# A decoder trunk's expert layer: 256 instead of 128 tokens gather their experts' rows, and wq, u and v are multiplied as plain float32

## The chip, the cores and the metric

One core of one Trainium2 chip runs the whole program. The metric is the device time of one execution in microseconds. The core has TensorE (PE, with its weight loads shown apart as PEld), VectorE (DVE), ScalarE (ACT), GpSimd (POOL), SyncE (SP) and 16 DMA engines that serve the queues of SP, ACT and POOL.

## The reference, cut to what matters

512 tokens of width 1024 go through two mixers (a gated recurrence and a sparse attention), then through the expert layer below, with an RMSNorm at the end. Each token picks, in each of 8 heads, 16 of 16384 experts; an expert is one row of u and one row of v.

```python
def block(xb):                                   # 128 tokens
    q = (xb @ w_q).reshape(TB, H, 2, PEER_HALF)  # 1024 -> 8 x 2 x 128
    s = jnp.einsum('thpc,phnc->thpn', q, sub_keys)
    s1, i1 = lax.top_k(s[:, :, 0], K)            # K = 16 of 128
    s2, i2 = lax.top_k(s[:, :, 1], K)
    cand = (s1[..., :, None] + s2[..., None, :]).reshape(TB, H, K * K)
    ...
    top_s, pos = lax.top_k(cand, K)
    eidx = ...                                   # i1 * 128 + i2 at pos: 128 experts a token
    g = jax.nn.softmax(top_s, axis=-1).reshape(TB, H * K)
    h = jnp.einsum('tkd,td->tk', u[eidx], xb)
    a = jax.nn.gelu(h, approximate=False) * g
    return jnp.einsum('tk,tkd->td', a, v[eidx])
```

## The kernel before

The mixers and the output projection take the first 465 us; they are the same in both kernels but for the last copies of the normalized activations. The expert layer follows, in two ways at once.

**Dense, for three blocks of 128 tokens (384 tokens).** Chunk j holds the 128 experts i * 128 + j. `u_chunk` loads the chunk of u (128 x 1024 float32, on SP's queue), multiplies it with the activations of all 384 tokens into one PSUM tile, and a Gelu writes h. `g_block` and `g_group` build the weight of every expert for every token from one-hot matrices (`oz`, `ow`), 8 tokens a group; each 32 tokens are written to HBM (`g_d`, on SP's queue). `v_parts` loads the chunk of v (ACT's queue) and the g of the chunk (one read serves QJ chunks), multiplies g and h to `aj`, and `v_product` adds aj times v into six PSUM accumulators (3 blocks x 2 halves of the width) that stay open to the end.

**Gathered, for block 0 (128 tokens).** `row` has POOL issue an indirect DMA, which fetches one row of 1024 float32 for each of 128 tokens. `u_row` multiplies it with the token and sums on DVE, `v_row` adds the weighted row of v to `acc` on DVE. 128 rows of u come before 128 rows of v. The row buffers (`gp`, 4 of them) let POOL run ahead of DVE by as many rows.

**Split products.** Most matmuls before are float32r products of two parts: `weight` loads a float32 tile, ACT casts a high part, DVE subtracts it for a low part, and `mm3` issues three matmuls (high x high, high x low, low x high). Products of plain float32 tiles, such as the scores of `scores`, are one call.

**Order.** The instructions of each engine stay in the order of the program. For each head: two `query` calls, UH[h] u chunks, the scores, then `picks` (top 16 on DVE). Next, u chunks up to LEAD with the groups of g between them. Then an iteration for each remaining chunk: u of chunk q + AHEAD, v of chunk q; after these, iterations with v alone for the first LEAD chunks, whose h was kept in HBM (`h_d`) till then. `some_rows` spreads the row operations: R0 for each u chunk in the heads, R1 while g is built, R2 in an iteration with u and v, R3 in one with v alone. It places them on DVE behind the instruction that `pace[0]` names; POOL takes them in the same order. `some_rows` takes rows of u only for heads that have picked. The last two chunks (`lasts`) come after all rows; `total` and `finish` add the residual, normalize and write.

Of the kernel before, what the change touches and what calls it, by code (L numbers as in the profile page):

```python
# [40 lines left out]
def trunk(ctx, tc, A, out, dbg=None):  # L41
# [41 lines left out]
    wst = ctx.enter_context(tc.tile_pool(name="wst", reuse_waits="tile", bufs=2))  # L83
# [504 lines left out]
    def norm_ffn(b):
        xf = xf0 if b == 0 else nf.tile([P, D], F32, name="xf")
# [41 lines left out]
    dve.tensor_copy(io16k, iota[:, :, None].to_broadcast([P, 16, 16]))  # L631

    def query(m, w=S):

        hi, lo = cut(weight(A["peer_wq"][m]), 8)
# [34 lines left out]
    def picks(h, sc2):  # L670
# [38 lines left out]
        dve.scalar_tensor_tensor(eidx[:, hs], e12[:, 0, 0], 128.0, e12[:, 1, 0], op0=OP.mult, op1=OP.add)  # L709
        for z in range(2):  # L710
            act.copy(iw12[:, :, z, hs], e12[:, z, 1:, :])

    def weigh():
# [7 lines left out]
        for b in range(NB):  # L721
            o = gw0 if b == 0 else iw12[:, b - 1, 2, :]
# [7 lines left out]

    LEAD, UH, AHEAD = 76, [3] * 7 + [7], 2
    UPRE = sum(UH)
    R0, R1, R2, R3, NOROW = 0, 1, 2.9, 0.95, 8
    TG, QJ = 32, 4
    NG = NT // TG
    g_d = dram.tile([NG, P, P, TG], F32, name="g_d")
# [12 lines left out]
    gp = ctx.enter_context(tc.tile_pool(name="gp", reuse_waits="tile", bufs=4))  # L749
    wk = ctx.enter_context(tc.tile_pool(name="wk4", reuse_waits="tile", bufs=2))  # L750
    hh = wk.tile([P, P], F32, name="hh", bufs=1)
    ah = wk.tile([P, P], F32, name="ah", bufs=1)
    scr = wk.tile([P, D], F32, name="scr", bufs=1)

    def row(tab, k):
        g = gp.tile([P, D], F32, name="row")
        pool.indirect_dma_start(out=g, out_offset=None, in_=A[tab],  # L757
                                in_offset=bass.IndirectOffsetOnAxis(ap=eidx[:, k:k + 1], axis=0))
        return g

# [12 lines left out]

    rows = list(range(P))
# [12 lines left out]

    vrows = []
    for h in range(8):
# [3 lines left out]
        for i, j in enumerate(range(sum(UH[:h]), sum(UH[:h + 1]))):  # L793
# [3 lines left out]
            some_rows(R0, h * 16)  # L797
# [7 lines left out]
    vt = ctx.enter_context(tc.tile_pool(name="vt", reuse_waits="tile", bufs=2))  # L805
    with ExitStack() as st:
# [8 lines left out]
        TB = 8  # L815
# [241 lines left out]
```

## Time and profile before

| | |
|---|---|
| time, median of 3 runs | 1710.43 us (1709.58 to 1716.81) |
| the profiled execution | 1711.65 us, of which the span of the profile is 1709.9 us |
| TensorE busy | 1675.5 us |
| DVE busy | 1340.8 us |
| ACT, POOL busy | 729.3 us, 377.0 us |
| moved by DMA | 414.9 MB |
| mean granted TensorE clock | 0.996 |

Busy times of TensorE come from modelled ends of pipelined matmuls: neighbours overlap, so what one costs in a row of many is the distance between two starts, not its length. The DMA share is the mean busy share of the 16 engines; GB/s is what they moved in the stretch.

### The profile page before, as it was taken

What the parts mean: (1) busy time and instruction counts of PE and PEld (TensorE: products, weight loads), DVE (VectorE), ACT (ScalarE), POOL (GpSimd) and SP (SyncE); (2) the same over time, 40 slices, a digit from 0 to 9 for tenths busy, and PEclk for the clock granted to TensorE, in tenths of its full rate; (3) what the DMA queues carried; (4) which work ended last, traced back from release to release, by engine and by line L of the source; (5) the groups of instructions that cost most, each with busy time, mean ns of one, the idle gap of its engine ahead of it and who ended that gap; (6) DMA issues with size and microseconds to landing.
All of it is one profiled execution on the core that took longest, in us unless ns stands there. A gap on an engine that the chain in (4) does not pass through costs nothing.

```text
span 1709.9 us, 24687 instructions
## 1 busy us (share of the span) xinstructions
PE 1675.5 (98%) x9095; PEld 1465.9 (86%) x9097; DVE 1340.8 (78%) x2573; ACT 729.3 (43%) x1052; POOL 377.0 (22%) x284
## 2 busy tenths in 40 slices
PE   8999999999999999999999999999999999999997
PEld 6988887777798888999999999999999978888886
DVE  4776887547699999998988588878887888877785
ACT  4322226734443434566666433333333333333333
POOL 2000000000010000232322144444444442333320
PEclk9999999999999999999999999999999999999999
DMA  7321233127454334798988899999999999999983
GB/s 234 131 81 50 75 125 116 56 94 241 163 177 128 126 123 131 248 359 316 359 316 336 278 338 335 337 331 319 322 317 344 324 336 353 357 333 346 321 299 131
DMA packets 172472, 414.90 MB, mean 243 GB/s; under 512 B 14744, under 2 KB 85784, under 8 KB 170688
## 3 DMA queue, kind: packets, MB, share of 16 engines
q10 hardware_dynamic: 101072, 141.70, 24.4%
q1 hardware_dynamic: 34416, 137.40, 22.6%
q0 software_dynamic: 36864, 134.23, 22.4%
q8 instruction: 71, 1.16, 0.3%
q14 instruction: 49, 0.40, 0.1%
HBM read 366.86 MB, written 49.04 MB: 243 GB/s over the span
## 4 chain that ended last, share of the span: by engine, by line
PE 41%; issue 33%; DMA 11%; POOL 9%; DVE 5%; ACT 1%; POOLq 0%; SPq 0%; ACTq 0%; DVEq 0%
POOL row L757 8%; PE acc L79 6%; PE acc L77 6%; PE acc L78 6%; DMA row<-in_peer_u,eidx 5%; PE ps_mm L77 5%; PE ps_mm L79 5%; PE ps_mm L78 5%; DMA row<-in_peer_v,eidx 4%; PE ps_hg L379 2%; PE ps_hg L77 1%; PE ps_yb L460 1%; PE ps_hg L78 1%; PE ps_hg L79 1%; DMA v_raw<-in_peer_v 1%
## 5 line engine op out<-in xcount | busy, mean ns | idle before, releaser
L108 ACT CAST w_hi<-w_raw 128x1024 fp32r<-128x1024 f32 (+2 forms) x215 | 219.2, 1020 | 401.0 <-PE ps_u L78 125.4
L110 DVE TENSOR_TENSOR w_lo<-w_raw,w_hi 128x1024 fp32r<-128x1024 f32 (+2 forms) x215 | 254.9, 1185 | 84.4 <-ACT w_hi L108 72.1
L757 POOL DMA_INDIRECT row<-in_peer_u,eidx x128 | 178.5, 1394 | 553.6 <-DVE hh L762 503.6
L77 PE MATMUL ps_u<-xfH,w_hi 128*128 128x384 f32 x800 | 274.0, 343 | 1.4 <-ACT hg L744 1.4
L78 PE MATMUL ps_u<-xfL,w_hi 128*128 128x384 f32 x800 | 270.6, 338 | 0.0
L79 PE MATMUL ps_u<-xfH,w_lo 128*128 128x384 f32 x800 | 269.9, 337 | 0.0
L757 POOL DMA_INDIRECT row<-in_peer_v,eidx x128 | 178.6, 1395 | 275.5 <-DVE acc L772 253.3
L78 PE MATMUL acc<-v_lo,aH 128*128 128x512 f32 x540 | 211.2, 391 | 3.3 <-DVE v_lo L895 3.3
L77 PE MATMUL acc<-v_hi,aH 128*128 128x512 f32 x540 | 212.1, 393 | 1.4 <-ACT aH L906 1.1
L79 PE MATMUL acc<-v_hi,aL 128*128 128x512 f32 x540 | 212.1, 393 | 0.1
L906 ACT CAST aH<-aj 128x384 fp32r<-128x384 f32 x128 | 65.6, 513 | 308.7 <-DVE aj L903 138.1
L772 DVE SCALAR_TENSOR_TENSOR acc<-row,ah,acc 128x1024 f32<-128x1024 f32 x127 | 162.6, 1281 | 21.4 <-DMA row<-in_peer_v,eidx 20.7
L762 DVE CUSTOM_DVE_ANT_0 scr<-row,xf 128x1024 f32<-128x1024 f32 x128 | 156.3, 1221 | 20.1 <-DMA row<-in_peer_u,eidx 19.3
L77 PEld LDWEIGHTS ps_u<-xfH,w_hi 128*128 128x128 f32 x800 | 150.2, 188 | 3.5 <-ACT hg L744 1.7
L78 PEld LDWEIGHTS ps_u<-xfL,w_hi 128*128 128x128 f32 x800 | 150.5, 188 | 2.2
L79 PEld LDWEIGHTS ps_u<-xfH,w_lo 128*128 128x128 f32 x800 | 150.2, 188 | 0.0
L895 DVE TENSOR_TENSOR v_lo<-v_raw,v_hi 128x1024 fp32r<-128x1024 f32 x90 | 110.0, 1223 | 24.1 <-ACT v_hi L894 23.5
L78 PEld LDWEIGHTS acc<-v_lo,aH 128*128 128x128 f32 x540 | 101.7, 188 | 24.0 <-DVE v_lo L895 3.6
L79 PEld LDWEIGHTS acc<-v_hi,aL 128*128 128x128 f32 x540 | 101.8, 188 | 23.2 <-DVE aL L908 0.8
L77 PEld LDWEIGHTS acc<-v_hi,aH 128*128 128x128 f32 x540 | 101.7, 188 | 22.1 <-ACT aH L906 1.4
L894 ACT CAST v_hi<-v_raw 128x1024 fp32r<-128x1024 f32 x90 | 94.4, 1048 | 51.6 <-PE acc L79 19.9
L858 ACT COPY stg<-ps_g 128x512 f32<-128x512 f32 x96 | 99.6, 1158 | 3.3 <-PE ps_g L855 3.3
(313 smaller groups left out, 3367.4 us busy)
## 6 DMA issues: line engine op xcount, KB each, us to landing
w_raw<-in_uT SPq DMA_DIRECT2D x128, 512.0 KB
v_raw<-in_peer_v ACTq DMA_DIRECT2D x90, 512.0 KB
g_d<-stg SPq DMA_DIRECT2D x12, 2048.0 KB
gj<-g_d ACTq DMA_DIRECT2D x32, 768.0 KB
w_raw<-in_peer_v ACTq DMA_DIRECT2D x38, 512.0 KB
w_raw<-in_wT SPq DMA_DIRECT2D x31, 512.0 KB
h_d<-hg ACTq DMA_DIRECT2D x76, 192.0 KB
hgr<-h_d ACTq DMA_DIRECT2D x76, 192.0 KB
```

The lines of the kernel that those rows point to most:

```text
L77: pe.matmul(ps, lh, rh, start=first, stop=False, **kw)
L78: pe.matmul(ps, lh, rl, start=False, stop=False, **kw)
L79: pe.matmul(ps, ll, rh, start=False, stop=last, **kw)
L108: act.copy(hi[:, :n], raw[:, :n])
L110: pace[0] = dve.tensor_tensor(lo[:, :n], raw[:, :n], hi[:, :n].bitcast(F32), op=OP.subtract)
L757: pool.indirect_dma_start(out=g, out_offset=None, in_=A[tab], in_offset=bass.IndirectOffsetOnAxis(ap=eidx[:, k:k + 1], axis=0))
L762: dve.tensor_tensor_reduce(out=scr, in0=row("peer_u", k), in1=xf0, scale=1.0, scalar=0.0, op0=OP.mult, op1=OP.add, accum_out=hh[:, k:k + 1])
L772: dve.scalar_tensor_tensor(acc, row("peer_v", k), ah[:, k:k + 1], acc, op0=OP.mult, op1=OP.add)
L858: act.copy(stg[:, :, t4:t4 + 4].rearrange("p j t -> p t j"), ps)
L894: act.copy(vh, raw)
L895: pace[0] = dve.tensor_tensor(vl, raw, vh.bitcast(F32), op=OP.subtract)
L906: act.copy(aH, gj)
```

## The change

Two blocks (NA = 2, 256 tokens) are gathered, two (256 tokens) are dense. wq, u and v are multiplied as they are loaded, in plain float32, one call instead of `mm3`; the activations are kept once (`xfT`) instead of in two parts, and neither the weights nor aj are split. h of all chunks stays on chip (`hst`, LEAD + 3 buffers). LEAD is 52 instead of 76, every head has 4 u chunks, u and v tiles have 4 buffers each, rows 6, and one read of g serves 8 chunks. Rows of u are taken head by head, both blocks in turn; rows of v block by block. Rows that are left when the loop over the chunks ends are issued together, before the last two chunks. The sum of the residual is written over x2.

```diff
+    NA = 2
+    NT = (NB - NA) * P
...
-            cs = slice(c4 * 4, c4 * 4 + 4)
-            dh = xfH[:, cs, b * P:(b + 1) * P]
-            act.copy(dh, ps)
-            dve.tensor_tensor(xfL[:, cs, b * P:(b + 1) * P], ps, dh.bitcast(F32), op=OP.subtract)
+            act.copy(xfT[:, c4 * 4:c4 * 4 + 4, b * P:(b + 1) * P], ps)
...
+    LEAD, UH = 52, [4] * 8
+    UPRE = sum(UH)
+    R0, R1, R2, R3, NOROW = 1.5, 0.9, 4.1, 2.05, 4
+    TG, QJ, TB = 32, 8, 8
+    NG = NT // TG
+    ust = ctx.enter_context(tc.tile_pool(name="ust", reuse_waits="tile", bufs=4))
+    hst = ctx.enter_context(tc.tile_pool(name="hst", reuse_waits="tile", bufs=1))
+    gp = ctx.enter_context(tc.tile_pool(name="gp", reuse_waits="tile", bufs=6))
...
+    def raw_weight(src):
+        raw = ust.tile([P, 1024], F32, name="u_raw")
+        sync.dma_start(raw, src)
+        return raw
...
     def query(m, w=S):
-        hi, lo = cut(weight(A["peer_wq"][m]), 8)
+        raw = raw_weight(A["peer_wq"][m]).rearrange("p (c m) -> p c m", c=8)
...
-                mm3(ps[:, ts], (hi[:, c, :], lo[:, c, :]), (xfH[:, c, ts], xfL[:, c, ts]), c == 0, c == 7)
+                pe.matmul(ps[:, ts], raw[:, c, :], xfT[:, c, ts], start=(c == 0), stop=(c == 7))
...
-    LEAD, UH, AHEAD = 76, [3] * 7 + [7], 2
-    R0, R1, R2, R3, NOROW = 0, 1, 2.9, 0.95, 8
-    TG, QJ = 32, 4
-    h_d = dram.tile([LEAD, P, NT], F32, name="h_d")
...
     def u_chunk(j, ps):
-        hi, lo = cut(weight(A["uT"][j]), 8)
+        raw = raw_weight(A["uT"][j]).rearrange("p (c m) -> p c m", c=8)
         for c in range(8):
-            mm3(ps[:, :NT], (hi[:, c, :], lo[:, c, :]), (xfH[:, c, P:], xfL[:, c, P:]), c == 0, c == 7)
-        hgt = wst.tile([P, NT], F32, name="hg", bufs=AHEAD + 2)
-        act.activation(hgt, ps[:, :NT], AF.Gelu)
-        if j < LEAD:
-            act.dma_start(h_d[j], hgt)
-        return hgt
+            pe.matmul(ps[:, :NT], raw[:, c, :], xfT[:, c, NA * P:], start=(c == 0), stop=(c == 7))
+        hts[j] = hst.tile([P, NT], F32, name="hg", bufs=LEAD + 3)
+        act.activation(hts[j], ps[:, :NT], AF.Gelu)
...
+    urows = [(b, h * 16 + k) for h in range(8) for b in range(NA) for k in range(16)]
+    vrows = [(b, k) for b in range(NA) for k in range(P)]
     due = [0]
-    def some_rows(rate, avail=P):
+    def some_rows(rate, heads=8):
         due[0] += rate
         with tc.issue_after(pace[0].ins):
             while due[0] >= 1:
                 due[0] -= 1
-                if rows and rows[0] < avail:
-                    u_row(rows.pop(0))
-                elif not rows and vrows:
-                    v_row(vrows.pop(0))
+                if urows:
+                    if urows[0][1] < heads * 16:
+                        u_row(*urows.pop(0))
+                elif heads > 8 and vrows:
+                    v_row(*vrows.pop(0))
...
+    def v_parts(j):
+        raw = vs.tile([P, D], F32, name="v_raw", bufs=4)
         act.dma_start(raw, v3[:, j, :])
...
+        aj = vs.tile([P, NT], F32, name="aj")
+        hgt = hts.pop(j)
+        pace[0] = dve.scalar_tensor_tensor(aj.rearrange("p (g t) -> p g t", t=TG), gq_t[0][:, :, j % QJ, :], 1.0 / 16384,
+                                           hgt.rearrange("p (g t) -> p g t", t=TG), op0=OP.mult, op1=OP.mult)
+        return aj, raw
     def v_product(b, n, a, v, first, last):
-        bs = slice(b * P, (b + 1) * P)
-        ns = slice(n * 512, (n + 1) * 512)
-        mm3(accs[b][n], (a[0][:, bs], a[1][:, bs]), (v[0][:, ns], v[1][:, ns]), first, last)
+        pe.matmul(accs[b][n], a[:, b * P:(b + 1) * P], v[:, n * 512:(n + 1) * 512], start=first, stop=last)
...
     for q, j in enumerate(order[:-2]):
         if LEAD + AHEAD + q < P:
-            ahead.append(u_chunk(LEAD + AHEAD + q, up.tile([P, 512], F32, name="ps_u")))
-        a, v = v_parts(j, ahead.pop(0) if ahead else None)
-        for b in range(3):
+            u_chunk(LEAD + AHEAD + q, up.tile([P, 512], F32, name="ps_u"))
+        a, v = v_parts(j)
+        for b in range(NB - NA):
             for n in range(2):
                 v_product(b, n, a, v, q == 0, False)
-        some_rows(R2 if q < P - LEAD else R3)
-        if q == P - 6:
-            last_rows()
-    if 0 not in fin:
-        last_rows()
-    lasts = [v_parts(j, None) for j in order[-2:]]
+        some_rows(R2 if q < P - LEAD else R3, 9)
+        rows_done()
+    some_rows(len(urows) + len(vrows) + 1, 9)
+    rows_done()
+    lasts = [v_parts(j) for j in order[-2:]]
```

## Rows read from the trace of the kernel before

**Rows 1.** The page, busy us (share of the span) and instructions of each engine.

```profile
PE 1675.5 (98%) x9095; PEld 1465.9 (86%) x9097; DVE 1340.8 (78%) x2573; ACT 729.3 (43%) x1052; POOL 377.0 (22%) x284
```

**Rows 2.** Busy us of each engine by stage, TensorE clock, DMA share, GB/s.

```profile
core 0: us, PE busy (x) PEld busy (x) DVE busy (x) ACT busy (x) POOL busy (x), PEclk, DMA share, GB/s
465.00:690.00 225.00, 219.74 (x1190) 199.45 (x1189) 211.26 (x934) 94.38 (x139) 4.29 (x4) 1.00 0.42 137
690.00:985.00 295.00, 290.15 (x2134) 278.78 (x2133) 242.27 (x271) 181.97 (x223) 80.34 (x52) 1.00 0.88 319
985.00:1372.00 387.00, 387.00 (x1948) 352.34 (x1947) 313.06 (x394) 134.09 (x185) 178.64 (x133) 1.00 0.93 328
1372.00:1660.00 288.00, 284.40 (x1227) 231.07 (x1226) 234.05 (x280) 101.94 (x141) 93.82 (x68) 0.99 0.98 341
```

**Rows 3.** The chain that ended last: start us, us, what was waited for.

```profile
1094.27 8.51 DMA row<-in_peer_u,eidx
...
1177.44 10.31 DMA row<-in_peer_u,eidx
```

**Rows 4.** DMA queues, 990 to 1190 us: packets, MB, share of 16 engines.

```profile
q0 software_dynamic: 10038, 36.57, 51.6%
q10 hardware_dynamic: 12768, 17.30, 25.2%
q1 hardware_dynamic: 3417, 12.42, 17.2%
```

**Rows 5.** Columns as in rows 2, for two stretches of 25 us and one of 5.

```profile
1410.00:1435.00 25.00, 24.92 (x109) 19.98 (x108) 20.78 (x26) 8.06 (x12) 4.99 (x5) 1.00 1.00 351
...
1485.00:1510.00 25.00, 25.00 (x111) 20.34 (x110) 19.90 (x24) 8.79 (x12) 6.18 (x7) 1.00 1.03 377
1015.00:1020.00 5.00, 5.00 (x27) 4.52 (x26) 2.58 (x5) 1.43 (x2) 1.87 (x2) 1.00 1.03 415
```

**Rows 6.** TensorE in order of time (start us, us), and two groups with mean ns.

```profile
13.35 2.84 PE L148 MATMUL ps_tr<-sq,ones 128*128 128x512 f32 x6
...
471.13 1.05 PE L652 MATMUL ps_tr<-kT,qT 128*128 128x128 f32 x8
...
800.03 0.34 PE L78 MATMUL ps_u<-xfL,w_hi 128*128 128x384 f32 x1
800.21 0.34 PE L79 MATMUL ps_u<-xfH,w_lo 128*128 128x384 f32 x1
...
802.50 1.09 PE L855 MATMUL ps_g<-ow,oz 128*128 128x128 f16 x16
...
1500.04 0.39 PE L77 MATMUL acc<-w_hi,aH 128*128 128x512 f32 x1
...
1500.27 0.39 PE L78 MATMUL acc<-w_lo,aH 128*128 128x512 f32 x1
...
L652 PE MATMUL ps_tr<-kT,qT 128*128 128x128 f32 x128 | 16.8, 274 | 0.0
...
L148 PE MATMUL ps_tr<-sq,ones 128*128 128x512 f32 x16 | 8.2, 632 | 3.4 <-ACT sq L147 3.4
```

**Rows 7.** Groups by line: xcount, busy us, mean ns, idle before.

```profile
L110 DVE TENSOR_TENSOR w_lo<-w_raw,w_hi 128x1024 fp32r<-128x1024 f32 x191 | 233.1, 1220 | 80.8 <-ACT w_hi L108 68.6 <-PE ps_g L855 10.5 <-issue 1.5
L757 POOL DMA_INDIRECT row<-in_peer_v,eidx x128 | 178.6, 1395 | 275.5 <-DVE acc L772 253.3 <-issue 10.3 <-DVE hh L762 5.6
...
L762 DVE CUSTOM_DVE_ANT_0 scr<-row,xf 128x1024 f32<-128x1024 f32 x128 | 156.3, 1221 | 20.1 <-DMA row<-in_peer_u,eidx 19.3
...
L845 DVE TENSOR_TENSOR oz<-io,i 128x2048 f16<-128x2048 f16 x48 | 58.5, 1219 | 0.0
```

**Rows 8.** DMA issues: line engine op xcount, KB each.

```profile
w_raw<-in_uT SPq DMA_DIRECT2D x128, 512.0 KB
...
g_d<-stg SPq DMA_DIRECT2D x12, 2048.0 KB
...
h_d<-hg ACTq DMA_DIRECT2D x76, 192.0 KB
```

More of the change, by code (lines that the diff above doesn't have):

```diff
@@ L756, in row, with u_row @@
+        act.activation(hts[j], ps[:, :NT], AF.Gelu)
+    def row(tab, b, k):
         g = gp.tile([P, D], F32, name="row")
         pool.indirect_dma_start(out=g, out_offset=None, in_=A[tab],
-                                in_offset=bass.IndirectOffsetOnAxis(ap=eidx[:, k:k + 1], axis=0))
+                                in_offset=bass.IndirectOffsetOnAxis(ap=eidx[:, b, k:k + 1], axis=0))
         return g
-    def u_row(k):
-        dve.tensor_tensor_reduce(out=scr, in0=row("peer_u", k), in1=xf0, scale=1.0, scalar=0.0, op0=OP.mult,
-                                 op1=OP.add, accum_out=hh[:, k:k + 1])
+    def u_row(b, k):
+        dve.tensor_tensor_reduce(out=scr, in0=row("peer_u", b, k), in1=xfa[:, b, :], scale=1.0, scalar=0.0, op0=OP.mult,
+                                 op1=OP.add, accum_out=hh[:, b, k:k + 1])
@@ L764, in u_row, with v_row @@
         if k == P - 1:
-            act.activation(ah, hh, AF.Gelu)
-            dve.tensor_tensor(ah, ah, gw0, op=OP.mult)
-    def v_row(k):
+            act.activation(ah[:, b, :], hh[:, b, :], AF.Gelu)
+            dve.tensor_tensor(ah[:, b, :], ah[:, b, :], gwa[:, b, :], op=OP.mult)
+    acc = {}
+    def v_row(b, k):
         if k == 0:
-            dve.tensor_scalar(acc, row("peer_v", k), ah[:, k:k + 1], None, op0=OP.mult)
-        else:
-            dve.scalar_tensor_tensor(acc, row("peer_v", k), ah[:, k:k + 1], acc, op0=OP.mult, op1=OP.add)
@@ L774, in trunk @@
-    rows = list(range(P))
+            acc[b] = wk.tile([P, D], F32, name="acc%d" % b, bufs=1)
+            dve.tensor_scalar(acc[b], row("peer_v", b, k), ah[:, b, k:k + 1], None, op0=OP.mult)
+        else:
+            dve.scalar_tensor_tensor(acc[b], row("peer_v", b, k), ah[:, b, k:k + 1], acc[b], op0=OP.mult, op1=OP.add)
+    urows = [(b, h * 16 + k) for h in range(8) for b in range(NA) for k in range(16)]
+    vrows = [(b, k) for b in range(NA) for k in range(P)]
     due = [0]
-    def some_rows(rate, avail=P):
+    def some_rows(rate, heads=8):
@@ L796, in trunk @@
                 sc2.append(scores(q1))
-            some_rows(R0, h * 16)
+            some_rows(R0, h)
         picks(h, sc2)
@@ L860, in trunk @@
         stgs = [None]
-        work = [(b, t0) for b in range(3) for t0 in range(0, P, TB)]
+        work = [(b, t0) for b in range(NB - NA) for t0 in range(0, P, TB)]
         state = {}
@@ L876, in trunk @@
     vp = ctx.enter_context(tc.tile_pool(name="vp", reuse_waits="tile", bufs=1, space=PSUM))
-    acc = vs.tile([P, D], F32, name="acc", bufs=1)
-    accs = [[vp.tile([P, 512], F32, name="acc_%d_%d" % (b, n)) for n in range(2)] for b in range(3)]
+    accs = [[vp.tile([P, 512], F32, name="acc_%d_%d" % (b, n)) for n in range(2)] for b in range(NB - NA)]
     v3 = A["peer_v"].rearrange("(i j) d -> i j d", j=P)
+    gfin = vs.tile([P, D], F32, name="gfin", bufs=1)
+    act.dma_start(gfin, bass.AP(tensor=A["norm_final"].tensor, offset=A["norm_final"].offset, ap=[[0, P], [1, D]]))
@@ L920, in total @@
         if n == 0:
[L921 to L922 removed]
+            fin[b] = [vs.tile([P, 2, 512], F32, name="o_fin", bufs=2), vs.tile([P, 2], F32, name="ss")]
+        g, ss = fin[b]
         ns = slice(n * 512, (n + 1) * 512)
[L924 to L926 removed]
+        xs = x2[:, b, ns]
+        dve.tensor_tensor(xs, src, xs, op=OP.add)
+        act.activation(scr[:, ns], xs, AF.Square, accum_out=ss[:, n:n + 1])
+        dve.tensor_tensor(g[:, n, :], xs, gfin[:, ns], op=OP.mult)
     def finish(b):
[L930 removed]
+        g, ss = fin[b]
         dve.tensor_tensor(ss[:, 0:1], ss[:, 0:1], ss[:, 1:2], op=OP.add)
@@ L938, in trunk, with rows_done @@
     order = list(range(LEAD, P)) + list(range(LEAD))
-    vrows = list(range(P))
-    ahead = [u_chunk(j, up.tile([P, 512], F32, name="ps_u")) for j in range(LEAD, LEAD + AHEAD)]
-    def last_rows():
-        while vrows:
-            v_row(vrows.pop(0))
-        for n in range(2):
-            total(0, acc[:, n * 512:(n + 1) * 512], n)
-        finish(0)
+    AHEAD = 2
+    for j in range(LEAD, LEAD + AHEAD):
+        u_chunk(j, up.tile([P, 512], F32, name="ps_u"))
+    def rows_done():
+        for b in range(NA):
+            if b not in fin and not urows and not any(r[0] == b for r in vrows):
+                for n in range(2):
+                    total(b, acc[b][:, n * 512:(n + 1) * 512], n)
+                finish(b)
     for q, j in enumerate(order[:-2]):
         if LEAD + AHEAD + q < P:
-            ahead.append(u_chunk(LEAD + AHEAD + q, up.tile([P, 512], F32, name="ps_u")))
-        a, v = v_parts(j, ahead.pop(0) if ahead else None)
-        for b in range(3):
+            u_chunk(LEAD + AHEAD + q, up.tile([P, 512], F32, name="ps_u"))
+        a, v = v_parts(j)
+        for b in range(NB - NA):
             for n in range(2):
                 v_product(b, n, a, v, q == 0, False)
-        some_rows(R2 if q < P - LEAD else R3)
-        if q == P - 6:
-            last_rows()
-    if 0 not in fin:
-        last_rows()
-    lasts = [v_parts(j, None) for j in order[-2:]]
-    for b in range(3):
+        some_rows(R2 if q < P - LEAD else R3, 9)
[3 more added lines that the diff above has]
+    lasts = [v_parts(j) for j in order[-2:]]
+    for b in range(NB - NA):
         for n in range(2):
```

95 lines of the change are left out of this document (29 added, 66 removed).

## The prediction

> **What bounds the kernel now.** I read the busy line of the page first, and in it TensorE: 98% busy, no other engine above 78% [rows 1]. An average hides the stages, so next come four stretches cut at the expert part: routing (465 to 690 us), building the weights g (690 to 985), u and v products together (985 to 1372), v products alone (1372 to 1660) [rows 2]. The reader should see two columns: TensorE is busy 98 to 100% in each of them, and the DMA share climbs 0.42, 0.88, 0.93, 0.98. So TensorE sets the time, and from 690 us on the DMA engines are almost as full. That the second resource is really queueing and not just lightly occupied is seen in the chain of waits: a gathered row that is waited for takes 8.5 to 10.3 us from issue to landing [rows 3], though its 524 kB are only 1.5 us of the engines at 350 GB/s.
>
> **What the engines can move.** This number carries the forecast. In 990 to 1190 us the rows moved 36.57 MB in 51.6% of 200 us, that is 354 GB/s of engine time; u alone 12.42 MB in 17.2%, 361; v with the weights g 343 [rows 4]. Stretches of 25 us whose share is about full moved 351 and 377 GB/s, and a lucky 5 us moved 415 [rows 5]. The new traffic has fewer short pieces (h leaves, g is read 1 kB at a time instead of 512 B), so I take 370 GB/s, between the two 25 us rows and nearer the upper; the ends are 351 and 415.
> The Trainium skill (HBM Reference, Specifications) says that a core streaming alone measures about 425 GB/s, and its share is 358 only when its partner streams as well. No row here of 5 us or more on the plain loads and rows holds 425; by that figure the sum below would be 1704 us.
>
> **TensorE's part.** Split products go out as one instruction each: neighbours start 0.18 us apart with 384 columns and 0.23 us with 512 [rows 6]. Plain float32 goes out as two instructions per product: 8 in 1.05 us with 128 columns, 6 in 2.84 us with 512 [rows 6]. Taking off one's own length (0.27 and 0.63) leaves 0.11 and 0.44 us from start to start, in proportion to the columns, so 256 columns take 0.22. At 128 columns the spacing is still that of the columns, so loading weights is hidden and costs nothing extra at 256.
> - u chunk: before 24 x 0.176 = 4.2 us; after 8 x 2 x 0.22 = 3.55 us, for 256 tokens instead of 384.
> - v chunk: before 18 x 0.23 = 4.15 us; after 2 blocks x 2 halves x 2 x 0.44 = 3.5 us.
> - 16 queries of 512 tokens: before 24 x 0.23 x 16 = 88 us, after 16 x 0.44 x 16 = 113 us. Plain float32 loses here, since no token leaves.
>
> **The other engines.** The splits leave DVE and ACT (the low part of a chunk is 1.2 us of DVE [rows 7]); instead DVE has 512 row operations of about as much [rows 7], 4.1 an iteration, 5.1 us, plus some 0.4 us for the product of g and h: under any iteration below. POOL issues 512 gathers of 1.4 us [rows 7], 5.7 us an iteration. The work queued on DVE is in order: the aj of iteration q+1, which TensorE's v product needs, stands behind the rows of iteration q, so a late row stops TensorE.
>
> **Bytes, stage by stage.** A u, a v or a gathered row is 524 kB (512 KB in the issue list), a write of g 2.1 MB [rows 8]; h's 76 writes of 192 KB [rows 8], and as many reads, vanish.
> 1. Up to the first query, 465 us, nothing changes that matters: 8 subtractions of the xf split leave, the copies stay.
> 2. Routing: 16 queries 113, 32 u chunks 32 x 3.55 = 114, scores 128 x 0.11 = 14, idle as before 5: 246 us (225 before). DVE is 211 us busy there now [rows 2]; 43 low parts of 1.2 us leave and 42 rows of 1.3 come, so it stays just under. Only four u chunks follow the scores of head 7 instead of seven, some 14 us, and the picks of a head are (211 - 52) / 8 = 20 us of DVE, part of it begun earlier: I add 8 us. DMA needs 53 MB, 143 us: covered. End at 719.
> 3. Weights g: 20 u chunks 71 us, 32 groups of 16 products, 0.9 us each (1.09 in [rows 6], less the part that overlaps the next product), 29 us; DVE 32 x 2.44 [rows 7] + 14 rows 18 = 96; DMA 34.6 MB, 94 us. Three resources at 94 to 100: 105 us, and 6 for the hand-over of g through HBM (a write, then a read that waits for it). End at 830.
> 4. 76 iterations with u and v: TensorE 7.05 us. DMA: 0.524 x 2 + 0.131 (g) + 4.1 x 0.524 = 3.33 MB, at 370 GB/s 9.0 us. DMA is late: 253 MB.
> 5. 50 iterations of v alone: TensorE 3.5 us; 0.524 + 0.131 + 2.05 x 0.524 = 1.73 MB, 4.7 us. DMA again: 87 MB.
> 6. Left rows: given out are 7 heads x 4 x 1.5 = 42, 16 x 0.9 = 14, 76 x 4.1 = 312, 50 x 2.05 = 102, together 470 of 512. The 42 others come at once after the loop, 22 MB, on DVE ahead of the last two aj.
> Steps 4 to 6 are 363 MB with the last loads: 363 / 0.370 = 981 us. After the last row come its sum, two v chunks (7 us) and the output, as the 9 us after TensorE's last product now: 18 us.
> **Sum:** 830 + 981 + 18 = 1829 us of span. The profiled execution had 1709.9 us of span in 1711.65 us, 1.2 us above the median of 1710.43; with that around it I forecast **1831 us**, 7% slower. TensorE's gain, 0.65 us for each of 256 chunks less 25 us of queries, is real and buys nothing: 134 MB of rows come, 30 MB of h and 16 MB of g leave, so 89 MB more cost 240 us of the engines. Idle were 0.58 x 225 + 0.12 x 295 + 0.07 x 387 + 0.02 x 288 = 199 us in [rows 2], and 130 of these lie in routing, where few experts are known yet and 42 rows (60 us) go.
>
> **The rivals.**
> A. TensorE stays the bound; transfers are hidden. Then steps 4 and 5 take 76 x 7.05 + 50 x 3.5 = 711 us, the 42 rows about 60 (POOL's 1.4 us each), 830 + 711 + 60 + 18 = 1619, 1621 us with what lies around the span: 5% faster. For it: TensorE's 98 to 100% now, and that a share of 0.98 has not stopped it [rows 2]. Against: it asks 472 GB/s in step 4 (3.33 MB in 7.05 us), and nothing above 415 shows.
> B. The DMA engines, with 4 u, 4 v and 6 row buffers always asking, hold the rate of their best 5 us [rows 5]: 363 / 0.415 = 875, so 1725 us; the range 395 to 425 gives 1769 to 1704 us. The point that decides between slower and not slower is 422 GB/s over the whole second half: 363 / 0.422 = 860, 1710 us. The skill's 425 lies just beyond it (HBM Reference, above); the rows, so far, below. For it: the share of some stretches exceeds 1 and their rate with it. Against: rows landing after 8.5 to 10.3 us at only 328 GB/s.
> C. Slower still: rows keep to 345 to 350 GB/s, as in [rows 4], or TensorE, now idle a fifth of the time, is granted less than the 1.00 that it has in [rows 2] and falls behind in turn. At 350: 1037 + 850 = 1887 us.
>
> **How the numbers follow.** Forecast (355 to 390 GB/s, 1780 to 1872 us) 0.62; A 0.11; B 0.17, of which 0.03 under 1702, 0.04 within 0.5% and 0.10 over; C 0.10. Half a per cent (8.6 us) is about what a measurement of this kernel can tell from no change. So faster 0.14, same 0.04, slower 0.82. The range leaves out A, the fastest part of B and the slow half of C, 0.19 in all: 1715 to 1895 us.
>
> **What would show it.** Right: after 830 us a DMA share of 0.97 or more, TensorE busy about 80% and waiting for aj, DVE waiting for rows from both tables, 9.0 and 4.7 us an iteration, and a stretch of some 60 us near the end with rows and hardly a product. Wrong: over 400 GB/s through the u and v stage (B), TensorE above 95% there (A), u products further apart than 0.22 us (TensorE's part), or row operations on DVE done well ahead of aj.

## The result and the profile after

The changed kernel takes 1768.94 us (median of 4 runs, 1766.91 to 1770.52), the kernel before 1710.01 us (1706.93 to 1716.81): ratio 1.034, 95% interval 1.031 to 1.037. It is 59 us slower. The forecast was 1831 us, 121 us slower: the direction and the cause came out as told, the size was off by a factor of two.

The page of the kernel after: its engines, DMA share and GB/s in 40 slices of 44 us, its traffic, and the chain that ended last by engine.

```profile
PE 1544.0 (87%) x6388; PEld 1064.4 (60%) x6390; DVE 1234.9 (70%) x2517; ACT 356.2 (20%) x618; POOL 594.0 (34%) x540
...
DMA  6321242146366666699999999999999999999996
GB/s 235 124 75 57 78 150 90 48 130 186 116 248 209 233 204 230 230 331 345 391 389 404 394 408 405 394 407 403 397 406 399 389 381 399 405 369 341 379 355 253
DMA packets 154865, 503.15 MB, mean 285 GB/s; under 512 B 16104, under 2 KB 35944, under 8 KB 153616
...
DMA 34%; PE 27%; issue 25%; POOL 8%; DVE 5%; ACT 1%; SPq 0%; POOLq 0%; ACTq 0%; DVEq 0%
```

TensorE fell from 98% of a span of 1710 us [rows 1] to 87% of 1767, so 131 us less of it is busy, and yet the end comes later. From the 18th slice on the DMA share is 9 in every digit but the last: the DMA engines are busy through the whole second half. 503 MB go instead of 415.

Cut at the same events as before [rows 2], the stages of the kernel after are: routing, the weights g, u and v together, v alone, the rows that are left, the end (columns as in rows 2).

```profile
core 0: us, PE busy (x) PEld busy (x) DVE busy (x) ACT busy (x) POOL busy (x), PEclk, DMA share, GB/s
461.00:707.00 246.00, 239.29 (x935) 169.16 (x933) 209.25 (x959) 54.46 (x100) 52.14 (x48) 0.98 0.62 211
707.00:839.00 132.00, 123.51 (x918) 105.37 (x918) 96.00 (x110) 72.08 (x97) 23.54 (x14) 0.98 0.83 302
839.00:1451.00 612.00, 536.45 (x1732) 339.03 (x1733) 406.12 (x583) 28.44 (x75) 333.29 (x305) 0.93 1.02 399
1451.00:1694.00 243.00, 190.74 (x415) 82.06 (x413) 161.83 (x170) 2.06 (x5) 126.22 (x113) 0.91 0.98 378
1694.00:1752.00 58.00, 6.54 (x15) 2.58 (x14) 52.73 (x46) 0.00 (x0) 40.82 (x34) 0.59 0.90 332
1752.00:1767.00 15.00, 0.00 (x0) 0.00 (x0) 6.71 (x17) 5.95 (x15) 2.02 (x3) 0.50 0.29 105
```

In the two stages where before TensorE was at 99 to 100% and the DMA share at 0.93 and 0.98, the roles are exchanged: TensorE 88% (536 of 612) and 78% (191 of 243), DMA 1.02 and 0.98. Routing and the weights g end 146 us earlier than before (839 against 985); from there to the end it takes 928 us against 725.

DMA queues of the kernel after, 850 to 1230 us (columns as in rows 4):

```profile
q0 software_dynamic: 27026, 98.41, 65.5%
q10 hardware_dynamic: 12904, 30.58, 21.0%
q1 hardware_dynamic: 6336, 23.07, 15.4%
```

q0 carries the gathered rows. A packet of it took 0.655 x 380 us x 16 engines / 27026 = 147 ns of an engine; before it was 0.516 x 200 x 16 / 10038 = 164 ns [rows 4], for packets of the same mean size (3.64 kB). A packet took an engine less time in the kernel that has more rows on their way. This is what the forecast missed; the runs with fewer row buffers below show it.

What waits for what in the kernel after: groups of waits (us in total, times, longest), then three steps of the chain that ended last (start us, us).

```profile
DVE scr L763 <- DMA row<-in_peer_u,eidx: 139.6, 138, 6.5
...
DVE acc L776 <- DMA row<-in_peer_v,eidx: 104.0, 122, 2.2
...
PE acc L902 <- DMA v_raw<-in_peer_v: 94.7, 13, 9.2
```

```profile
930.07 15.07 DMA row<-in_peer_u,eidx
...
1526.04 19.35 DMA v_raw<-in_peer_v
1545.53 20.16 PE acc L902 x40
```

DVE waits for rows of both tables, 244 us in all (for rows of u 140 us, 19 before [rows 7]), and a row that ends a wait was on its way for up to 15 us (8.5 to 10.3 in [rows 3]; the longest on the chain before took 12). TensorE itself is stopped by late v chunks, 19 us on their way. In the u and v stage it waits 45 us for v and 20 us for aj, where the prediction had looked for aj alone (group of products, 839 to 1451 us: busy us, mean ns, idle before):

```profile
L902 PE MATMUL acc<-v_raw,aj 128*128 128x512 f32 x596 | 294.6, 641 | 69.3 <-DMA v_raw<-in_peer_v 45.1 <-DVE aj L897 20.2 <-issue 4.0
```

### The profile page after: what moved, and what is told of

Read it like the earlier page. It is cut to its first block, busy times and chain, and to the rows that moved or that the text cites. A ratio compares the mean times of both kernels' runs of the same rounds, so it can differ in the third digit from the quotient of the medians.

```text
span 1767.0 us, 19063 instructions
## 1 busy us (share of the span) xinstructions
PE 1544.0 (87%) x6388; PEld 1064.4 (60%) x6390; DVE 1234.9 (70%) x2517; ACT 356.2 (20%) x618; POOL 594.0 (34%) x540
## 4 chain that ended last, share of the span: by engine, by line
DMA 34%; PE 27%; issue 25%; POOL 8%; DVE 5%; ACT 1%; SPq 0%; POOLq 0%; ACTq 0%; DVEq 0%
DMA row<-in_peer_u,eidx 16%; DMA row<-in_peer_v,eidx 12%; POOL row L758 7%; PE ps_mm L77 5%; PE acc L902 5%; PE ps_mm L79 5%; PE ps_mm L78 4%; DMA v_raw<-in_peer_v 4%; DVE scr L763 2%; PE ps_hg L380 2%; DVE acc L776 1%; PE ps_yb L461 1%; PE ps_hg L77 1%; PE ps_hg L79 1%; PE ps_hg L78 1%
## 5 line engine op out<-in xcount | busy, mean ns | idle before, releaser
L902 PE MATMUL acc<-v_raw,aj 128*128 128x512 f32 x1024 | 491.6, 633 | 121.8 <-DMA v_raw<-in_peer_v 94.7
L758 POOL DMA_INDIRECT row<-in_peer_u,eidx x256 | 283.5, 1108 | 486.7 <-DVE hh L763 397.1
L902 PEld LDWEIGHTS acc<-v_raw,aj 128*128 128x128 f32 x1024 | 205.2, 204 | 369.3 <-issue 291.0
L763 DVE CUSTOM_DVE_ANT_0 scr<-row,xfa 128x1024 f32<-128x1024 f32 x256 | 313.8, 1226 | 145.2 <-DMA row<-in_peer_u,eidx 139.6
L776 DVE SCALAR_TENSOR_TENSOR acc<-row,ah,acc 128x1024 f32<-128x1024 f32 x254 | 326.1, 1284 | 108.6 <-DMA row<-in_peer_v,eidx 104.0
L752 PE MATMUL ps_u<-xfT,u_raw 128*128 128x256 f32 x1536 | 356.4, 385 | 14.2 <-ACT hg L754 14.2
L758 POOL DMA_INDIRECT row<-in_peer_v,eidx x256 | 291.3, 1138 | 223.5 <-DVE acc L776 167.6
L752 PEld LDWEIGHTS ps_u<-xfT,u_raw 128*128 128x128 f32 x1536 | 292.8, 193 | 85.8 <-issue 33.7
L752 PE MATMUL ps_hg<-xfT,u_raw 128*128 128x256 f32 x512 | 116.4, 386 | 3.4 <-ACT hg L754 3.4
L659 PE MATMUL ps_mm<-xfT,u_raw 128*128 128x512 f32 (+1 forms) x288 | 111.9, 546 | 0.0
```

Source lines behind the costliest of these rows:

```text
L659: pe.matmul(ps[:, ts], raw[:, c, :], xfT[:, c, ts], start=(c == 0), stop=(c == 7))
L752: pe.matmul(ps[:, :NT], raw[:, c, :], xfT[:, c, NA * P:], start=(c == 0), stop=(c == 7))
L763: dve.tensor_tensor_reduce(out=scr, in0=row("peer_u", b, k), in1=xfa[:, b, :], scale=1.0, scalar=0.0, op0=OP.mult, op1=OP.add, accum_out=h ...
L776: dve.scalar_tensor_tensor(acc[b], row("peer_v", b, k), ah[:, b, k:k + 1], acc[b], op0=OP.mult, op1=OP.add)
L902: pe.matmul(accs[b][n], a[:, b * P:(b + 1) * P], v[:, n * 512:(n + 1) * 512], start=first, stop=last)
```

## The experiments

**Theory:** the DMA engines set the time from the weights g on, as the prediction says; TensorE's gain is real and lies idle. **Rivals:** plain float32 costs TensorE more than its instruction spacing tells; the row operations on DVE, which works in order, set the pace, not the bytes; the short pieces of g do. And, for the size of the miss, a theory that came after the result and before these runs: what the engines can move depends on how much is asked of them at once, so the kernel before could not show it.

**The rows' bytes alone taken away.** The row of block 0 is used for block 1 too: 256 gathers go, all 512 row operations of DVE stay.

```diff
     def row(tab, b, k):
-        g = gp.tile([P, D], F32, name="row")
+        if b:
+            return last_row[0]
+        g = last_row[0] = gp.tile([P, D], F32, name="row")
...
-    urows = [(b, h * 16 + k) for h in range(8) for b in range(NA) for k in range(16)]
-    vrows = [(b, k) for b in range(NA) for k in range(P)]
+    urows = [(b, k) for k in range(P) for b in range(NA)]
+    vrows = [(b, k) for k in range(P) for b in range(NA)]
```

> The changed kernel, but each gathered row of block 0 is used for block 1 too (block 1 then adds the wrong experts): 256 gathers instead of 512, while DVE has the same 512 row operations in another order and TensorE the same products. Theory 1, the DMA engines set the time from 830 us on: 134 MB less, 120 MB of them after 830 us, leaves 243 MB, 609 us at 399 GB/s, less than TensorE's 711 us; so TensorE takes over and the time falls to 1620 to 1660 us. Rival, DVE's order sets it (aj stands behind the row operations, whose number is the same): above 1730 us. Rival, plain float32 costs TensorE more than it gains: above 1730 us too.

Measured 1586.77 us, 0.928 of before (0.925 to 0.931). The stage with u and v (columns as in rows 2):

```profile
850.00:1330.00 480.00, 480.00 (x1677) 318.27 (x1676) 385.89 (x563) 27.11 (x71) 235.19 (x149) 1.00 0.93 333
```

TensorE is busy all of the 480 us and its clock is back at 1.00, with the same products in the same form and every operation of DVE; a DMA share of 0.93 stops nothing here. So neither plain float32 nor DVE's order held the kernel up. (The edit halves POOL's gathers too; POOL, busy 333 of the 612 us in the kernel after, was not at its limit.) TensorE's side of the change is worth 1709 - 1587 = 122 us, and the 134 MB of the second block's rows take 1769 - 1587 = 182 us. The time lies 33 us below the range expected, although TensorE takes over as told: from the first v product (838 us) to the last one of the loop (1520 us) it needs 682 us in place of 711, and the rows left then hold it for 49 us, where rival A had 60.

**TensorE's work taken away.** Half of u's products are left out from chunk 52 on.

```diff
-        for c in range(8):
-            pe.matmul(ps[:, :NT], raw[:, c, :], xfT[:, c, NA * P:], start=(c == 0), stop=(c == 7))
+        n = 8 if j < LEAD else 4
+        for c in range(n):
+            pe.matmul(ps[:, :NT], raw[:, c, :], xfT[:, c, NA * P:], start=(c == 0), stop=(c == n - 1))
```

> The changed kernel, but from chunk 52 on a u chunk is multiplied over half of its inner blocks only (4 of 8, the others left out), all loads unchanged: 76 x 1.78 = 135 us less of TensorE in the stage with u and v. Theory 1 (DMA engines): within 10 us of the changed kernel's 1769 us. Rival, TensorE (products in plain float32, or their lower clock) sets the stage: about 1640 us.

Measured 1779.94 us, ratio 1.040 (1.038 to 1.043). Some 130 us less of TensorE (76 x 4 products of 0.43 us) bought nothing and cost 11 us. Two stretches, the u and v stage and the last 125 us:

```profile
850.00:1365.00 515.00, 409.89 (x1141) 226.93 (x1140) 311.48 (x503) 27.51 (x72) 251.15 (x233) 0.89 1.02 398
1640.00:1765.00 125.00, 0.00 (x0) 0.00 (x0) 107.86 (x85) 0.00 (x0) 96.33 (x84) 0.50 0.97 353
```

The rate of the stage is what it was (398 GB/s against 399). TensorE is done earlier, at 1632 us instead of 1701, and 89 rows, not 30, are still to be gathered then; they go at 353 GB/s, beside a DVE that is busy 108 of the 125 us. Together with the first experiment this settles that TensorE's work doesn't set the time. The edit also changed DVE's order: the last aj stands ahead of 99 row operations, in the kernel after ahead of 39. That this is what costs the 11 us was not tried.

**Row buffers: 3 and 4 in place of 6.** The same bytes and the same products, fewer rows on their way at once. 4 is the number of the kernel before.

```diff
-    gp = ctx.enter_context(tc.tile_pool(name="gp", reuse_waits="tile", bufs=6))
+    gp = ctx.enter_context(tc.tile_pool(name="gp", reuse_waits="tile", bufs=3))
```

> The changed kernel with 3 row buffers instead of 6, bytes unchanged. The changed kernel moved 399 GB/s in the u and v stage where I had taken 370. Theory A, the rate comes from more requests waiting at the engines: with 3 rows in flight of 9 to 10 us each the rate falls to 330 to 370 GB/s and the time rises by 60 to 150 us, to 1830 to 1920 us. Theory B, the rate comes from fewer short pieces: the same time within 15 us.

> The changed kernel with 4 row buffers, the number of the kernel before; bytes unchanged. By theory A (the rate comes from requests waiting; 3 buffers moved 296 GB/s at a share of 0.86, 6 moved 399 at 1.02): about 340 to 360 GB/s and 1860 to 1930 us. This would say that my 370 was a rate of 4 buffers. Rival, only fewer than 4 starve the engines: 1770 to 1800 us.

Measured 2109.54 us with 3 (ratio 1.234, 1.229 to 1.239) and 1921.48 us with 4 (1.123, 1.116 to 1.129). The u and v stage and q0 in the same stretch, first with 3, then with 4:

```profile
880.00:1680.00 800.00, 576.71 (x1693) 346.89 (x1692) 389.11 (x562) 27.29 (x72) 309.97 (x293) 0.86 0.86 296
...
q0 software_dynamic: 42310, 154.07, 56.5%
```

```profile
880.00:1500.00 620.00, 495.21 (x1518) 302.34 (x1517) 350.66 (x522) 24.60 (x65) 291.55 (x265) 0.91 0.95 344
...
q0 software_dynamic: 38009, 138.39, 61.6%
```

| row buffers | GB/s in the stage | DMA share | GB/s ÷ share | ns of an engine per packet of q0 |
|---|---|---|---|---|
| 3 | 296 | 0.86 | 344 | 171 |
| 4 | 344 | 0.95 | 362 | 161 |
| 6 (the change) | 399 | 1.02 | 391 | 147 |
| 8 (below, with g in float16) | 405 | 1.02 | 397 | 147 |

The last column is worked out as above: share of q0 x length x 16 / packets. The fourth column is what the prediction took for the capacity of the engines. It is none: it grows with the buffers. With 4 row buffers the changed kernel shows 362, about what the kernel before, also with 4, shows (328 / 0.93 = 353 [rows 2]) and what I extrapolated to 370; with 6 it isn't the same number any more. With 3 buffers I had expected a far smaller loss: the rows then move at 154.07 MB / 800 us = 193 GB/s, which is 3 x 0.524 MB in 8.2 us, about the time that a row was on its way before [rows 3]. So with 3 buffers the round trip of a row looks like the bound, and the engines idle for 14% of the stage.

**Shorter pieces of g** (512 B instead of 1 KB per piece, as in the kernel before):

```diff
-    TG, QJ, TB = 32, 8, 8
+    TG, QJ, TB = 32, 4, 8
```

> The changed kernel with a read of g for 4 chunks instead of 8, so in pieces of 512 B instead of 1 kB, as in the kernel before; bytes unchanged. Theory A (requests waiting): within 10 us of 1769 us. Theory B (short pieces hold the engines): the rate falls back towards 370 GB/s, about 60 us more, 1830 us.

Measured 1779.84 us, ratio 1.041 (1.039 to 1.044), 11 us more, at 395 GB/s in the u and v stage in place of 399. The piece size is worth something, but it isn't what parts 370 from 399.

**h through HBM again**, for the 52 chunks that are kept longest:

```diff
-        hts[j] = hst.tile([P, NT], F32, name="hg", bufs=LEAD + 3)
+        hts[j] = hst.tile([P, NT], F32, name="hg", bufs=4)
         act.activation(hts[j], ps[:, :NT], AF.Gelu)
+        if j < LEAD:
+            act.dma_start(h_d[j], hts.pop(j))
...
-        hgt = hts.pop(j)
+        if j < LEAD:
+            hgt = vs.tile([P, NT], F32, name="hgr")
+            act.dma_start(hgt, h_d[j])
+        else:
+            hgt = hts.pop(j)
```

> The changed kernel with one part undone: h of the first 52 chunks goes through HBM, as before (52 writes and 52 reads of 131 kB). Theory 1 (bytes over the DMA engines' rate): the 6.8 MB of writes fall before 830 us, where the engines have idle time, the 6.8 MB of reads behind it at 399 GB/s: 17 us more, about 1786 us. Rival: the traffic is hidden, as in the kernel before, and the time stays within 5 us of 1769. Rival: the read delays aj each time, 40 us or more.

Measured 1787.49 us, ratio 1.045 (1.040 to 1.050): some 18 us more than the change (ratio 1.034), for 6.8 MB of reads in the full half (17 us at 399 GB/s). In the profiled executions 14 of them lie behind the first v product (942 us against 928) and 4 ahead of it (843 us against 839). So bytes put into the saturated part cost about their time at its rate, and 6.8 MB of writes ahead of it 4 us at most.

**One block gathered**, the rest of the change kept:

```diff
-    NA = 2
+    NA = 1
...
-    LEAD, UH = 52, [4] * 8
+    LEAD, UH = 40, [4] * 8
...
-    R0, R1, R2, R3, NOROW = 1.5, 0.9, 4.1, 2.05, 4
+    R0, R1, R2, R3, NOROW = 0.75, 0.9, 2.1, 1.3, 4
...
-    gp = ctx.enter_context(tc.tile_pool(name="gp", reuse_waits="tile", bufs=6))
+    gp = ctx.enter_context(tc.tile_pool(name="gp", reuse_waits="tile", bufs=4))
```

> One part alone: one block gathered (128 tokens, 384 dense, as before), but wq, u and v in plain float32 and h on chip (40 chunks ahead, 4 row buffers, row rates halved). TensorE by the distances between starts: routing 113 + 32 x 5.2 + 14 + 13, weights g 120 (48 groups on DVE), 88 x 10.4 with u and v, 38 x 5.2 with v, 18 at the end: 461 + 306 + 120 + 915 + 198 + 18 = 2018 us; the DMA engines are asked for about 230 GB/s. Theory 1: 1990 to 2050 us, TensorE above 95% busy, DMA share under 0.75 with u and v. Rival, the plain products cost no more than split ones: near 1710 us.

Measured 2014.45 us, ratio 1.177 (1.171 to 1.183). From the middle of the run:

```profile
950.00:1780.00 830.00, 830.00 (x2255) 428.18 (x2254) 250.85 (x342) 39.55 (x81) 231.37 (x170) 1.00 0.67 226
```

TensorE is the only bound here, DMA at 0.67. So the two halves of the change pull against each other: without the second block the rest of it costs 304 us, with TensorE as the bound (plain float32 takes two instructions of 0.43 us for 512 columns, against three split ones of 0.23 [rows 6]). The second gathered block then gives back 245 of them by taking its tokens off TensorE, until the rows' bytes take over as the bound. (LEAD, the row rates and the row buffers were fitted to one block; they were not tried apart.)

**Rows begun earlier**, to use the idle DMA time of routing (share 0.62):

```diff
-    R0, R1, R2, R3, NOROW = 1.5, 0.9, 4.1, 2.05, 4
+    R0, R1, R2, R3, NOROW = 2.5, 1.7, 4.1, 2.05, 4
```

> The changed kernel with more rows early: 2.5 instead of 1.5 rows a u chunk while the experts are picked, 1.7 instead of 0.9 while g is built; everything else the same. 28 + 13 rows, 21.5 MB, move into stages whose DMA share is 0.62 and 0.83. Theory 1: the time behind them shrinks by 21.5 MB at 399 GB/s, 54 us, and the stretch of rows alone at the end vanishes, while DVE in the routing stage goes from 209 to 245 of 246 us and may cost up to 10 us: 1710 to 1730 us. Rival, DVE in routing is the bound and takes back what is gained: 1750 us or more.

Measured 1763.14 us, ratio 1.032 (1.027 to 1.037). The expected gain didn't come. The end of routing in this kernel:

```profile
705.00:740.00 35.00, 22.11 (x95) 16.88 (x94) 33.01 (x137) 6.50 (x12) 11.29 (x10) 0.84 0.65 236
```

DVE is busy 33 of 35 us while TensorE waits: with the additional rows DVE becomes the bound of routing, the first u chunk of the g stage moves from 707.7 to 738.6 us and the first v product from 839 to 880.6. From there to the end it takes 878 us instead of 928, 50 us less and near the 54 expected, but that part starts 42 us later. What the engines gained early was paid back on DVE. The idle DMA time of routing isn't free to use.

**Fewer bytes of g.** g is rounded to float16 (it is no longer the float32 of the reference), read 16 chunks at a time; 8.4 MB of writes and as many of reads leave.

```diff
-    g_d = dram.tile([NG, P, P, TG], F32, name="g_d")
+    g_d = dram.tile([NG, P, P, TG], F16, name="g_d")
...
-    TG, QJ, TB = 32, 8, 8
+    TG, QJ, TB = 32, 16, 8
...
-                act.copy(stg[:, :, t4:t4 + 4].rearrange("p j t -> p t j"), ps)
+                act.activation(stg[:, :, t4:t4 + 4].rearrange("p j t -> p t j"), ps, AF.Copy, scale=0.25)
```

> The changed kernel with the weights g rounded to float16 on their way through HBM (a quarter of the scale, so that the sum of eight fits), one read for 16 chunks, so the pieces stay 1 kB: 8.4 MB less written and 9.4 MB less read (the 17th read goes too). Theory 1 (bytes over the engines' rate): the reads save 9.4 MB / 399 GB/s = 24 us behind 839 us; of the writes' 21 us some stay hidden as now, since the share is 0.83 there: 1730 to 1750 us. Rival: small transfers hide and the time stays within 10 us of 1769.

Measured 1797.53 us, ratio 1.049 (1.046 to 1.052): slower than the change itself. The next kernel keeps this and adds 8 row buffers, LEAD 48, the rates 1.6, 2.0, 4.1, 2.6 and, to make room, fewer buffers for three tiles of the routing:

> e9 with 8 row buffers instead of 6, h of 48 chunks instead of 52 kept (no read of g twice), rows 1.6 a chunk while experts are picked, 2.0 while g is built and 2.6 with v alone, so that no rows are left at the end. Behind about 825 us: 446 rows, 80 u, 128 v and 8.4 MB of g, 351 MB. If 8 buffers raise the rate to 410 GB/s (3, 4 and 6 gave 296, 344 and 399): 825 + 856 + 15 = 1696 us, faster than both kernels by a little. If the rate stays at 395: 1730 us.

Measured 1757.13 us, ratio 1.026 (1.023 to 1.028), not the forecast either. Both kernels have the same new cost, the copy of the g sums from PSUM on ACT. Its group in the kernel after, in the first of these two, and in the last kernel below:

```profile
L862 ACT COPY stg<-ps_g x64: 1042/1100/1145, 718.9 to 818.2; 128x512 f32<-128x512 f32 x64
```

```profile
L862 ACT ACTIVATE stg<-ps_g x64: 2397/2754/2838, 720.5 to 883.1; 128x512 f16<-128x512 f32 x64
```

```profile
L862 ACT ACTIVATE stg<-ps_g x64: 592/596/598, 720.1 to 819.8; 128x512 f16<-128x512 f32 x64
```

(ns: shortest, median, longest; start of the first and last, us.) The same number of elements took 1.10 us as 4-byte writes 128 B apart, 2.75 us as 2-byte writes 64 B apart, and 0.60 us in the last kernel, which writes four neighbours, 8 B, in a row. With 64 copies of 2.75 us ACT became the bound of the g stage, whose last copy starts at 883 us instead of 818.

**The order of that copy turned round**, all else as in the kernel of 1757 us:

```diff
-                act.activation(stg[:, :, t4:t4 + 4].rearrange("p j t -> p t j"), ps, AF.Copy, scale=0.25)
+                act.activation(stg[:, :, t4:t4 + 4], ps.rearrange("p t j -> p j t"), AF.Copy, scale=0.25)
```

> e10 but for the order in which ACT writes g as float16: four tokens of an expert next to each other (8 bytes in a row) instead of one token over all experts (2 bytes every 64). In e9 and e10 that copy took 2.75 us instead of 1.10 and the stage of g ended at 893 instead of 829 us. If the scattered 2-byte writes cost the time, the copy falls to 1.2 us or less, the first read of g comes at 825 to 835 us, and with the 866 us that e10 took from its first read of g to its end the time is 1690 to 1705 us, a little under the kernel before. If the float16 type alone costs it, nothing changes: 1757 us.

Measured **1700.67 us**, ratio 0.993 (0.991 to 0.996): as expected. It is the one version with all gathers that is clearly ahead of both kernels, of the one before by 0.7% and of the change by 3.9%. Its u and v stage:

```profile
835.00:1440.00 605.00, 544.70 (x1793) 343.75 (x1794) 414.74 (x579) 28.77 (x76) 343.07 (x311) 0.96 1.02 405
...
q0 software_dynamic: 44413, 161.75, 67.4%
```

**The rounding done by the DMA instead**, with the float32 staging of the change and 7 row buffers:

```diff
-                    sync.dma_start(g_d[b * (P // TG) + t0 // TG], stgs[0])
+                    pool.dma_start(g_d[b * (P // TG) + t0 // TG], stgs[0])
```

> e10 with g written by ACT in float32 as in the changed kernel and rounded to float16 by the transfer to HBM, issued by POOL; 7 row buffers, as float32 staging takes the room. The copy is 1.10 us again; the engines read 16.8 MB and write 8.4 MB in a stage with spare time. Behind the first read of g at about 830 us, 351 MB at 405 GB/s and 15 us: 1712 us; with the writes of g behind gathers on POOL up to 10 us more: 1700 to 1725 us. Rival: writes in POOL's queue wait behind gathers that wait for DVE, the stage of g ends 30 us or more later: above 1740 us.

Measured 1709.36 us, ratio 0.998 (0.997 to 1.000): no loss any more, and 9 us behind the kernel whose copy was turned round. The copy has the instruction of the slow one and writes float32 again:

```profile
L862 ACT ACTIVATE stg<-ps_g x64: 1035/1108/1150, 720.2 to 821.5; 128x512 f32<-128x512 f32 x64
```

1.11 us, so it is neither the other instruction nor (0.60 us above) float16 by itself that made the copy slow, but float16 in that order.

## Why the prediction was right in its cause and wrong in its size

| step | forecast | measured |
|---|---|---|
| routing ends | 719 us | 707 us |
| weights g end | 830 us | 839 us |
| u and v, 76 iterations | 684 us, 9.0 each, 370 GB/s | 612 us, 8.05 each, 399 GB/s |
| v alone, 50 iterations | 235 us, 4.7 each | 243 us, 4.9 each, 378 GB/s |
| rows left, then the end | 60 and 18 us | 58 and 15 us |
| bytes of the three stages | 363 MB | 612 x 0.399 + 243 x 0.378 + 58 x 0.332 = 355 MB |

**The step that failed** is "What the engines can move": 370 GB/s. Over the three stages it was 355 MB in 913 us, 389 GB/s, and 399 in the longest. Of the 62 us between the forecast span (1829) and the measured one (1767), 355 / 0.370 - 913 = 47 us are this term. Another 21 us are the 8 MB fewer that were left to move at 839 us: the g stage had moved 132 us x 302 GB/s = 40 MB against 34.6 forecast, and routing 52 against the 48 of its own loads and rows, since the u, v and row buffers fill ahead. 3 us are the end, and the g stage, which ends 9 us later than forecast, takes 9 back. The cause that was forecast, the rows' bytes at full DMA engines, held; this term was too low.

The rows that misled were right; the choice among them and my reading were not. I divided a rate by its share [rows 4] and took the quotient for a ceiling. The runs with 3, 4 and 6 row buffers show that the quotient itself rises with the number of rows on their way, from 344 to 391 GB/s, because a packet takes 171, 161, 147 ns. A share of 0.93 to 0.98 in a kernel with 4 row buffers was near full for that much asked, not for six. The 415 GB/s of a stretch of 5 us [rows 5] was nearer to what came; whether more was waiting in it was not looked up. Nor does "nothing above 415 shows" (rival A) hold for the whole trace of the kernel before. Two full stretches of its g stage, which carry writes of g and h besides loads and few rows, lie above 370, and 5 us of the first far above (columns as in rows 2):

```profile
760.00:785.00 25.00, 25.00 (x185) 24.50 (x183) 17.77 (x22) 15.78 (x22) 6.16 (x5) 1.00 1.00 378
810.00:835.00 25.00, 25.00 (x197) 24.21 (x196) 22.43 (x26) 16.24 (x21) 8.41 (x5) 1.00 0.98 381
760.00:765.00 5.00, 5.00 (x42) 4.85 (x39) 4.45 (x6) 3.29 (x5) 1.49 (x2) 1.00 1.06 448
```

Rival B had 0.17, and its range for 395 to 425 GB/s began at 1769 us. That the measured time falls on this edge is partly chance: 389 GB/s over the three stages is still within the forecast's 355 to 390, and the 8 MB fewer bring the time below its 1780 us. The diff had the fact that parts 370 from the measured rate in one line, row buffers 4 to 6, and I named it under B without pricing it.

**What held.**
- TensorE. A u chunk and a v chunk take 3.44 us each from start to start (forecast 3.55 and 3.5), as this stretch of the kernel after shows (start us, us):

```profile
1428.70 3.62 PE L752 MATMUL ps_u<-xfT,u_raw 128*128 128x256 f32 x16
1432.15 3.60 PE L902 MATMUL acc<-v_raw,aj 128*128 128x512 f32 x8
1435.59 3.62 PE L752 MATMUL ps_u<-xfT,u_raw 128*128 128x256 f32 x16
```

  That TensorE is busy for 536 of the 612 us, which is 76 x 7.05, is chance: the stage holds 71 u chunks and 74.5 v chunks, 500 us at this spacing. Its products last longer than in the run of the shared rows, where the clock is 1.00 (v: 641 ns on the mean against 598). Rival A fell: the stage is 76 us longer than TensorE's busy time.
- Routing: 246 us, the sum without the 8 us that I added for a pause on DVE, from 461 us on instead of 465. (I gave it 53 MB, but its own loads and rows are 48.) DVE is busy 209 of them; its low parts leave and rows come, as told, and the early rows above show how little room is left.
- The weights g took 132 us in place of 111, 9 us more than the early end of routing gained. The hand-over of g is 10 of them (its first read is issued at 829 us, the first v product starts at 839; 6 forecast). TensorE is busy 124 of the 132, where I had 100: 25 u chunks (400 instructions), not 20, stand ahead of the first v product, about five of them behind the last group of g, while g is handed over. The groups take 0.92 us from start to start, as told.
- The 42 rows left at the end: the length is right (58 us against 60) and the reason isn't. I priced them by bytes, but 46 operations, 39 of them rows of 1.28 us, keep DVE busy for 53 of the 58 us, and the DMA share is 0.90. Nor do they stand ahead of the last two aj, as the prediction and the description of the change have it: DVE takes the last aj at 1694.0 us and these 39 behind it. So DVE's order isn't that of the program everywhere, and no v chunk is left for the end, which took 15 us in place of 18:

```profile
1694.02 0.42 DVE L897 SCALAR_TENSOR_TENSOR aj<-gj,hg 128x256 f32<-128x256 f32 x1
1694.36 5.24 DVE L776 SCALAR_TENSOR_TENSOR acc<-row,ah,acc 128x1024 f32<-128x1024 f32 x4
...
1714.16 6.61 DVE L776 SCALAR_TENSOR_TENSOR acc<-row,ah,acc 128x1024 f32<-128x1024 f32 x5 [0.79 <-DMA row<-in_peer_v,eidx]
```

**Smaller misses.** In the stage of v alone TensorE doesn't wait a little in each iteration; it runs eight chunks (64 products) and then stands for 8 to 9 us for a v chunk:

```profile
1545.53 30.45 PE L902 MATMUL acc<-v_raw,aj 128*128 128x512 f32 x64 [9.24 <-DMA v_raw<-in_peer_v]
...
1584.28 29.84 PE L902 MATMUL acc<-v_raw,aj 128*128 128x512 f32 x64 [8.31 <-DMA v_raw<-in_peer_v]
```

Eight chunks are the period of the 1 MB read of g, which ACT issues into the same queue as v's loads. The other runs bear this out in part. With a read for 16 chunks (the kernel of 1700.67 us) the longest stands come 16 chunks apart (first two lines below). With a read of half the size for 4 chunks (the run with shorter pieces) they still come every eight, at every second read (third line). Why there only every second read delays v stays open.

```profile
1479.35 40.52 PE L902 MATMUL acc<-v_raw,aj 128*128 128x512 f32 x88 [11.83 <-DMA v_raw<-in_peer_v]
...
1554.07 61.09 PE L902 MATMUL acc<-v_raw,aj 128*128 128x512 f32 x136 [12.05 <-DMA v_raw<-in_peer_v]
```

```profile
1574.64 29.63 PE L902 MATMUL acc<-v_raw,aj 128*128 128x512 f32 x64 [7.71 <-DMA v_raw<-in_peer_v]
```

Of rival C one half came: TensorE, idle between products, was granted 0.93 and 0.91 of its clock in the two stages, against 1.00 and 0.99 before [rows 2]. It cost nothing that shows, as TensorE has time to spare there, and the clock is back at 1.00 in the u and v stage where the second block's rows are gone.

## What to carry to other kernels

A rate divided by its DMA share isn't what the engines can move. It belongs to the number of transfers on their way for which it was read: here 4 row buffers moved 344 GB/s and 6 moved 399. So before a change that also adds buffers is priced by bytes, run one of the two kernels with the other number, or let the range reach up to the fastest stretches of the old trace. And when work is taken off one engine at the price of bytes, add up the bytes in the stages that are already full alone: idle transfer time in an earlier stage counts only if the data is known there and the engine that consumes it has room.

## What the hardware showed that was not expected

- One core sustains 399 GB/s for 612 us of gathered rows, plain loads and short pieces together, and 405 over 605 us with 8 row buffers and g in float16. The fastest slices of the latter's page, 42 us each, hold 410. The Trainium skill (HBM Reference, Specifications (TRN2)) gives about 425 GB/s for a core that streams alone, and 358 as its share when its neighbour streams too. With one core at work 410 comes close to the first figure. The Trainium skill (DMA: Bandwidth & Descriptors, Where 436 GB/s comes from) says that for transfers between HBM and SBUF the 358 binds. That doesn't hold in these runs.
- The time of a gathered row's packet on an engine fell from 171 to 147 ns as the row buffers went from 3 to 6, and stayed there with 8 (with g in float16). The buffer count alone was changed between 3, 4 and 6; which part of the way gets faster stays open.
- ACT's copy of 128x512 elements out of PSUM took 1.10 us with 4-byte writes 128 B apart, 2.75 us with 2-byte writes 64 B apart and 0.60 us with runs of 8 B. Halving the bytes made the instruction 2.5 times slower until the order of the writes, and with it that of the reads, was changed.
